# Evictions in three steps, a level of a head in two, a reordered first stage, and a gate pair as the stream's last, in a hybrid recurrent and convolutional layer

## The chip, the core and the metric

The kernel runs on one NeuronCore of a Trainium2 chip. The metric is the device time of one execution in microseconds. The core's engines work side by side, each through its own queue in the order of the program: TensorE (PE in the profile; its weight loads are PEld), VectorE (DVE), ScalarE (ACT) and GpSimd (POOL) compute, and SyncE (SP) issues most DMAs. An engine whose next instruction waits does not look past it.

## What is computed

One layer on a prompt of 1024 tokens with 16 meta tokens ahead of it, and on 8 single-token samples with a stored state. The reference, cut:

```python
xn = rmsnorm(h, norm_pre)
proj = xn @ w_in                       # 1024 x (10 * 1024), ten sections
q, fr, i_in, z_a, b_g, c_g, h_c, z_b, gate_a, gate_b = split(proj)
f = lb + (1 - lb) * sigmoid(fr);  k = 1 - f;  qa = silu(q)
# per head (8 heads, 128 x 128 state), exactly causal:
#   S_t = diag(f_t) S_{t-1} + k_t v_t^T ;  o_t = q_t^T S_t      (v = i_in)
o = o * rsqrt(mean(o * o) + EPS) * hgrn_norm * silu(z_a);  y_a = o @ w_a
u = c_g * h_c;  conv = causal conv of width 3 over u
y_b = (b_g * conv * silu(z_b)) @ w_b
merged = sigmoid(gate_a) * y_a + sigmoid(gate_b) * y_b
h = h + rmsnorm(merged @ w_o, norm_post)
```

Products are made to nearly float32 accuracy: each operand is split into a high part (ACT, a cast) and a low part (DVE or POOL, a subtraction), and a product is three matmuls, high x high, high x low, low x high (`mm3`, lines 112 to 116).

## The kernel before

**First stage (lines 850 to 1000).** The tokens come in eight chunks of 128, the even ones by SP, the odd ones by an indirect DMA that POOL issues (`load_chunk`). For a chunk c: `square(c)` on ACT and `rsqrt` on POOL (lines 82 and 83), `normalise(c)` on DVE, `turns(c)` (eight transposes on PE), `highs(c)` on ACT and `lows(c)` on DVE. They fill the factors b11, b12, b21, b22. Beside them the first head's input and forget projections are made in the plain way, four column ranges each (`plain`, 24 matmuls or `mm3` x 8; its evictions are e1 and e2). Then `sums12(i)` on DVE (eight subtractions, line 219) and `sums34(i)` on POOL make the differences that the other factors are turned from.

**The stream (`strassen`, line 544).** All other projections go in 39 pairs of sections, by a scheme of seven products for a 2 x 2 block product. A pair has products j = 0 to 6, each of two column chunks c, so 14 chunks of 12 matmuls; "chunk" below means one of these. After a chunk's matmuls `flush()` runs what was put off into the list `later`, then the weights' high part (c = 0, ACT) or low part (c = 1, DVE) of the product after next is made, and the chunk's own eviction `after(...)` is put into `later`: it is issued one chunk on. At j = 0, 2, 4 it copies the bank to a slot `sc` (ACT, line 554); at j = 1, 4, 5, 6 it calls the pair's `evac`, with the copy as `s`, or with none (j = 5). `added` sums bank and copy on DVE (line 281). Two banks `ga`, two `gb` and four `h` are there; product j = 0 of the next pair takes the `ga` banks that j = 5 leaves (odd pairs from 25 on take `h` banks).

The order of pairs is `stream_of`: query and output gate of head 0, then for each further head a pair of merge gates, input and forget, query and output gate; then the eighth gate pair, then for m = 0 to 7 a `u_pair(m)` and a `b_pair(m)` of the convolution branch. A u pair's `end` puts off the convolution's taps: ACT line 698, DVE lines 700 to 708, which run in the first chunks of the b pair behind it.

**What is woven in.** `weave` emits the steps of a generator between the chunks: a step of weight w comes once its middle falls due on the scale of chunks. `hgrn(m)`, the recurrence of a head, has 23 steps over 42 chunks (`W_HG`): preparation, seven levels of a scan over blocks that double (line 421 on: matmuls L424, then DVE `kc` L426, an ACT copy, `place_scores`, DVE `xc` L432 and a product L434), the states, and per half g `read_half(g)` (PE, ACT squares, `rsqrt` on POOL), `scaled(g)` (DVE L503), `back(g)` (four transposes, PE L509) and `gated(g)` (DVE L514). `add` (line 570), three POOL operations for the next pair's weights, is issued in a pair at j = 4. `sample_steps` then spreads the eight samples' work over the 176 chunks from pair 25 on, ten steps for each head: among them two DVE multiplications of 128 x 1024 (L778, L782), their sum (L784) with its output DMA, and one step later eight small matmuls on the sum (L790). In the last pair `tail` adds `fill`: it loads the recurrence's results and splits them (ACT and DVE, 128 x 1032 each).

**The rest** (line 1038 on): the products with w_a, w_b and w_o, and the output. The change leaves it alone.

Of the kernel before, what the change touches and what calls it, by code (L numbers as in the profile page):

```python
# [19 lines left out]
HL = 524  # L20
# [12 lines left out]
def hybrid_step(ctx: ExitStack, tc: tile.TileContext,  # L33
# [254 lines left out]

    def i_out(m, h, c0, n, pt, s):
        out = of_head(m, "it", h, c0, n)  # L290
        if s is None:
            act.copy(out, pt)
        else:
            added(pt, s, out)

    def f_out(m, h, c0, n, pt, s):
        out = of_head(m, "f", h, c0, n)
        sigmoid(added(pt, s, out), n, out)
        act.activation(out=out, in_=out, func=AF.Identity, scale=omlb[:, m:m + 1], bias=lb[:, m:m + 1])

    def q_out(m, h, c0, n, pt, s):
        out = of_head(m, "x", h, c0, n)
        y = added(pt, s)
        sg = sigmoid(y, n)
        later.append(lambda: (vec if s is None else pool).tensor_tensor(out=out, in0=y, in1=sg, op=ALU.mult))

    def z_out(m, h, c0, n, pt, s):
        out = of_head(m, "zs", h, c0, n)
        y = added(pt, s)
        sg = sigmoid(y, n)  # L310
        later.append(lambda: vec.scalar_tensor_tensor(out=out, in0=y, scalar=hnorm, in1=sg, op0=ALU.mult, op1=ALU.mult))  # L311


    W_HG = [0.8, 1.7, 1.7, 1.8, 1.4, 1.2, 1.9, 3.3] + [3.2] * 5 + [2.2] + [0.8, 0.8, 0.8, 1.9, 1.9, 1.2, 1.2, 1.2, 1.2]

    def hgrn(m):
# [13 lines left out]
        turned(iT, V, 0)  # L330
# [7 lines left out]
        turned(iT, V, 1)  # L338
# [4 lines left out]
        ex = slot("ex", 24)  # L343
        pool.tensor_copy(cap(ex, 0, [[12, 2], [1, 12]]), cap(iT, 512, [[HL, 2], [1, 12]]))
# [69 lines left out]
        for l in range(7):  # L414
# [38 lines left out]
        place_scores(6, got)  # L453
        turned(K, KT, 0)
# [73 lines left out]
        scaled(1, *r1)  # L528
        b0 = back(0)
# [14 lines left out]
    def strassen(pairs, tail):  # L544
# [5 lines left out]
        def after(j, c, c0, n, o, of_c, held, evac, end):  # L550

            cols = slice(c0, c0 + n)
            if j in (0, 2, 4):
                act.copy(held[j][:, cols], o)  # L554
            if j == 1:
                evac(0, 0, c0, n, o, held[0][:, cols])
            if j == 4:
                evac(1, 1, c0, n, of_c[:, 0:n], held[4][:, cols])
            if j == 5:
                evac(1, 0, c0, n, o, None)  # L560
            if j == 6:
# [153 lines left out]
    def b_pair(m):  # L715
        def evac(r, h, c0, n, pt, s):
            t = conv[m][:, HY * h + c0:HY * h + c0 + n]
            y = added(pt, s)
            if r == 0:
                vec.tensor_tensor(out=t, in0=t, in1=y, op=ALU.mult)  # L720
            else:
                sg = sigmoid(y, n)

                def rest():
                    vec.tensor_tensor(out=sg, in0=y, in1=sg, op=ALU.mult)
                    vec.tensor_tensor(out=t, in0=t, in1=sg, op=ALU.mult)
                later.append(rest)
# [8 lines left out]
    def gate_pair(sec, m, dst):  # L736
        def evac(r, h, c0, n, pt, s):
            out = slot("cs", HL - 256)[:, 0:n] if s is None else s
            sigmoid(added(pt, s), n, out)
            sync.dma_start(dst[m + r][:, HY * h + c0:HY * h + c0 + n], out)  # L740
# [24 lines left out]
    N_SAMPLE = 10  # L765

    def sample_steps():
        loaded = sample_state(0)
        for m in range(8):
# [15 lines left out]
            sync.dma_start(hgrn_s_out[0, :, m].rearrange("b k v -> k b v"), sin.rearrange("p (b v) -> p b v", b=8))  # L785
            yield
# [60 lines left out]
    stream_of += [gates[7]] + [f(m) for m in range(8) for f in (u_pair, b_pair)]  # L847
# [39 lines left out]
    load_chunk(5)  # L887
    square(2)
    load_chunk(7)
    normalise(0)  # L890
    turns(0)
    square(1)
    normalise(2)
    highs(0)
    turns(2)
    lows(0)
# [25 lines left out]
    for kk in range(2):  # L922
        w_high(rf, wf, kk)
        w_low(rf, wf, kk)
    square(3)
    normalise(1)
    e1 = plain(wi, 0, *C0)
    turns(1)
    normalise(3)
    highs(1)  # L930
    turns(3)
    lows(1)
    e2 = plain(wf, 0, *C0)
    square(4)
    normalise(4)
    highs(3)
    lows(3)
    e1()
    turns(4)
    square(6)  # L940
    normalise(6)
    highs(4)
    lows(4)
    e2()
    e1 = plain(wi, 1, *C0)
    turns(6)
    square("s", 24)
# [10 lines left out]
    turns(5)  # L958
    square(7)
    normalise(7)  # L960
    highs(5)
    lows(5)
    e2()
# [4 lines left out]
    small_parts(s22, t2)  # L968
    highs(7)
    lows(7)  # L970
    e2 = plain(wf, 0, *C1)
    for i in range(4):
        sums12(i)
    next(stream)
    for i in range(4):
        sums34(i)
    e1()
    turn(1, 1)
    turn(3, 1)
    e2()  # L980
    e1 = plain(wi, 1, *C1)
# [243 lines left out]
```

## Time and profile before

| | |
|---|---|
| median of 3 runs | 1319.78 us (1318.26 to 1321.21) |
| profiled execution | 1319.05 us, its span 1317.2 us |
| PE busy | 1260.4 us, 96% |
| DVE, ACT, POOL busy | 844.3, 534.7, 406.1 us |
| first matmul of the stream | 60.37 us after the span's start |
| last matmul of the stream | 1029.86 us |
| mean granted TensorE clock | 0.991 |

Times below are microseconds from the span's start. A matmul's end is modelled, so short gaps can lie inside its bar: two pairs of one kind are best compared by their whole lengths. A granted clock under 1.00 in a stretch is the share of full speed (2.4 GHz) on average; 0.50 is the lower level, 1.2 GHz.

### The profile page before, as it was taken

The page shows a single profiled execution, that of the slowest core. Times are in us where ns is not written, and L with a number is a line of the kernel's source. Part 1 is how long each engine was busy: PE and PEld are TensorE (multiplying, and loading weights), DVE is VectorE, ACT ScalarE, POOL GpSimd, SP SyncE. Part 2 cuts the span into 40 slices and gives each one's busy share as a digit, 9 for nine tenths or more (in the row PEclk, how much of TensorE's full clock was granted, in tenths as well). Part 3 has the DMA queues.
Part 4 walks back from the last instruction along what each step waited for, and adds up shares of the span by engine and source line. Part 5 has one row for each costly group of instructions (what it writes and reads, how often), then busy time and mean ns, then how long its engine had stood idle before and what let it go on. Part 6 is the DMA issues. An engine that isn't in the chain of part 4 may idle for free. (4 is left out here: it accounts for less than half of the span.)

```text
span 1317.2 us, 25325 instructions
## 1 busy us (share of the span) xinstructions
PE 1260.4 (96%) x10041; PEld 1221.6 (93%) x10041; DVE 844.3 (64%) x1412; ACT 534.7 (41%) x1280; POOL 406.1 (31%) x502
## 2 busy tenths in 40 slices
PE   6899999999999999999999999899998999999997
PEld 5789999999999999999999999899998999999876
DVE  5878586685858668585785777676576523546052
ACT  6454555555455545445543333333334312313031
POOL 5634242433324242342522544344344000000010
PEclk9899999999999999999999999899999999999999
DMA  7012031221203122130222434242326633522041
GB/s 219 9 48 76 27 105 41 63 69 59 82 27 97 49 59 73 46 94 28 79 60 78 149 96 137 64 138 81 112 71 209 222 97 98 177 96 83 16 162 56
DMA packets 146500, 117.11 MB, mean 89 GB/s; under 512 B 6641, under 2 KB 130650, under 8 KB 146382
## 3 DMA queue, kind: packets, MB, share of 16 engines
q1 hardware_dynamic: 145806, 113.40, 28.1%
q0 software_dynamic: 576, 2.10, 0.4%
q8 instruction: 79, 1.29, 0.4%
q14 instruction: 39, 0.32, 0.1%
HBM read 89.48 MB, written 25.96 MB: 88 GB/s over the span
## 5 line engine op out<-in xcount | busy, mean ns | idle before, releaser
L595 DVE TENSOR_TENSOR w<-wq,w 128x512 fp32r<-128x512 f32 x153 | 125.0, 817 | 28.2 <-ACT w L589 27.5
L589 ACT CAST w<-sm 128x512 fp32r<-128x512 f32 x117 | 72.1, 616 | 150.4 <-PE gb L116 126.7
L281 DVE TENSOR_TENSOR sc<-gb,sc 128x256 f32<-128x256 f32 (+1 forms) x144 | 60.2, 418 | 68.8 <-ACT sc L554 66.3
L595 DVE TENSOR_TENSOR w<-sm,w 128x512 fp32r<-128x512 f32 x117 | 84.1, 719 | 29.7 <-ACT w L589 29.7
L589 ACT CAST w<-wq 128x512 fp32r<-128x512 f32 x156 | 96.3, 618 | 15.7 <-PE h L116 14.6
L599 POOL TENSOR_TENSOR sm<-wq,sm 128x512 f32<-128x512 f32 x39 | 60.6, 1554 | 136.1 <-DVE w L595 118.2
L114 PE MATMUL gb<-s1h,w 128*128 128x256 f32 (+2 forms) x344 | 100.7, 293 | 0.0
L114 PE MATMUL gb<-s3h,w 128*128 128x256 f32 (+2 forms) x328 | 95.7, 292 | 3.6 <-DVE sc L281 2.5
L554 ACT COPY sc<-ga 128x256 f32<-128x256 f32 x192 | 71.7, 374 | 66.6 <-PE ga L116 65.1
L115 PE MATMUL gb<-s1l,w 128*128 128x256 f32 (+2 forms) x344 | 97.7, 284 | 0.0
L575 POOL TENSOR_TENSOR sm<-wq 128x512 f32<-128x512 f32 x39 | 57.7, 1481 | 120.7 <-DVE w L595 95.2
L114 PE MATMUL gb<-s6h,w 128*128 128x256 f32 (+2 forms) x328 | 94.4, 288 | 0.0
L1138 POOL TENSOR_TENSOR st<-st,half 128x1 f32<-128x1 f32 (+1 forms) x9 | 5.0, 551 | 286.8 <-DVE st L1136 283.9
L115 PE MATMUL gb<-s3l,w 128*128 128x256 f32 (+2 forms) x328 | 93.2, 284 | 0.0
L115 PE MATMUL gb<-s6l,w 128*128 128x256 f32 (+2 forms) x328 | 92.4, 282 | 0.0
L116 PE MATMUL gb<-s3h,w 128*128 128x256 f32 (+3 forms) x312 | 89.0, 285 | 1.6 <-DVE w L595 1.5
L116 PE MATMUL gb<-s1h,w 128*128 128x256 f32 (+3 forms) x312 | 88.7, 284 | 0.5 <-DVE w L595 0.5
L116 PE MATMUL gb<-s6h,w 128*128 128x256 f32 (+3 forms) x312 | 88.2, 283 | 0.0
L114 PE MATMUL ga<-s0h,w 128*128 128x256 f32 (+3 forms) x288 | 83.1, 289 | 1.2 <-DVE zs L311 1.2
L114 PE MATMUL ga<-s2h,w 128*128 128x256 f32 (+3 forms) x272 | 80.5, 296 | 2.1 <-ACT sc L554 2.1
L115 PE MATMUL ga<-s0l,w 128*128 128x256 f32 (+3 forms) x288 | 81.2, 282 | 0.0
L114 PE MATMUL ga<-s5h,w 128*128 128x256 f32 (+3 forms) x256 | 74.9, 293 | 3.8 <-ACT sc L554 1.7
(748 smaller groups left out, 4692.4 us busy)
## 6 DMA issues: line engine op xcount, KB each, us to landing
wq<-in_w_in_dram SPq DMA_DIRECT2D x160, 256.0 KB
oz<-zs SPq DMA_DIRECT2D x16, 258.0 KB
ob<-zs SPq DMA_DIRECT2D x8, 516.0 KB
x<-ga SPq DMA_DIRECT2D x8, 516.0 KB
x<-gb SPq DMA_DIRECT2D x8, 516.0 KB
wq<-in_w_a_dram SPq DMA_DIRECT2D x16, 256.0 KB
wq<-in_w_b_dram SPq DMA_DIRECT2D x16, 256.0 KB
wq<-in_w_o_dram SPq DMA_DIRECT2D x16, 256.0 KB
```

Source lines behind the costliest of these rows:

```text
L114: pe.matmul(pt, wh, xh, start=first, stop=False, skip_group_check=onto)
L115: pe.matmul(pt, wh, xl, start=False, stop=False, skip_group_check=onto)
L116: pe.matmul(pt, wl, xh, start=False, stop=last, skip_group_check=onto)
L281: vec.tensor_tensor(out=out, in0=pt, in1=s, op=ALU.add)
L554: act.copy(held[j][:, cols], o)
L575: pool.tensor_tensor(out=s3, in0=a11, in1=a21, op=ALU.subtract)
L589: act.copy(w[:, 0:512], source(i))
L595: (pool if j in pairs[p][2] else vec).tensor_tensor(out=w[:, 512:1024], in0=source(i), in1=w[:, 0:512].bitcast(F32), op=ALU.subtract)
L599: pool.tensor_tensor(out=s2, in0=raws[p, 0, 1], in1=s2, op=ALU.subtract)
L1138: pool.tensor_tensor(out=rs[0:rows], in0=rs[0:rows], in1=half[0:rows, 0:1], op=ALU.pow)
```

## The change

- **Three steps.** A new `silu` puts the sigmoid off by one more chunk and the multiplication by another one: sum, sigmoid and multiplication of an eviction now come in three successive flushes. It serves query, output gate and the b pairs' r = 1; the sigmoids of forget gate and merge gates (with their DMA) are put off by one chunk too. The query's multiplication, on POOL before, is on DVE. At j = 4, `evac` comes one chunk after the copy that it needs.
- **Heads.** A level is two steps: matmuls, `kc` and `place_scores`; then the copy, `xc` and L434. Both halves of V, and the small copy `ex`, come in the first step; the placing of the last level, and `back(0)`, are steps of their own. 32 steps with new weights.
- **Samples.** Eleven steps for a head: an empty one between the sum and the matmuls.
- **Order of the stream.** The eighth gate pair moves from ahead of the u and b pairs to the end.
- **First stage.** Squares are issued earlier, the odd chunks 5 and 7 are both loaded ahead of the second square, `normalise(1)` comes ahead of `lows(2)`, the lower bounds' small operations later, two of the four `sums12` ahead of a plain product.

```diff
+    def silu(y, n, use):
+        def first():
+            sg = sigmoid(y, n)
+            later.append(lambda: use(sg))
+        later.append(first)
...
     def f_out(m, h, c0, n, pt, s):
         out = of_head(m, "f", h, c0, n)
-        sigmoid(added(pt, s, out), n, out)
-        act.activation(out=out, in_=out, func=AF.Identity, scale=omlb[:, m:m + 1], bias=lb[:, m:m + 1])
+        y = added(pt, s, out)
+        def gate():
+            sigmoid(y, n, out)
+            act.activation(out=out, in_=out, func=AF.Identity, scale=omlb[:, m:m + 1], bias=lb[:, m:m + 1])
+        later.append(gate)
...
-        sg = sigmoid(y, n)
-        later.append(lambda: (vec if s is None else pool).tensor_tensor(out=out, in0=y, in1=sg, op=ALU.mult))
+        silu(y, n, lambda sg: vec.tensor_tensor(out=out, in0=y, in1=sg, op=ALU.mult))
...
-    W_HG = [0.8, 1.7, 1.7, 1.8, 1.4, 1.2, 1.9, 3.3] + [3.2] * 5 + [2.2] + [0.8, 0.8, 0.8, 1.9, 1.9, 1.2, 1.2, 1.2, 1.2]
+    W_HG = [2.6, 1.7, 1.7, 1.8, 1.4, 1.2, 1.9, 1.7, 1.9] + [2.2, 1.3] * 5 + [1.2, 1.2] + [0.6, 0.8, 0.8, 0.8, 1.9, 1.9, 1.2, 1.2, 0.8, 1.2, 1.2]
...
             vec.tensor_tensor(out=kc, in0=kc, in1=cap(eb, eo + 1, [[2, nb], [hb - 1, 2], [0, B]]), op=ALU.mult)
+            if l:
+                place_scores(l - 1, last)
+            yield
             if l < 6:
                 ko = 512 * ((l + 1) % 2)
                 act.copy(comp(kms, ko, nb // 2, 2 * B, 2 * B), comp(K, 0, nb // 2, HL + 2 * B, 2 * B))
-            if l:
-                place_scores(l - 1, last)
...
         scaled(1, *r1)
+        yield
         b0 = back(0)
...
             if j == 4:
-                evac(1, 1, c0, n, of_c[:, 0:n], held[4][:, cols])
+                later.append(lambda: evac(1, 1, c0, n, of_c[:, 0:n], held[4][:, cols]))
...
-    N_SAMPLE = 10
+    N_SAMPLE = 11
...
             sync.dma_start(hgrn_s_out[0, :, m].rearrange("b k v -> k b v"), sin.rearrange("p (b v) -> p b v", b=8))
+            yield
             yield
...
-    stream_of += [gates[7]] + [f(m) for m in range(8) for f in (u_pair, b_pair)]
+    stream_of += [f(m) for m in range(8) for f in (u_pair, b_pair)] + [gates[7]]
...
     square(0)
     load_chunk(5)
+    load_chunk(7)
     square(2)
-    load_chunk(7)
     normalise(0)
...
     highs(2)
+    normalise(1)
     lows(2)
+    square(3)
+    for kk in range(2):
+        w_high(rf, wf, kk)
+        w_low(rf, wf, kk)
+    e1 = plain(wi, 0, *C0)
...
+    square(5)
+    square(7)
+    e2()
+    flush()
     e2 = plain(wf, 1, *C0)
-    square(5)
     normalise(5)
     s11, s12, s21, s22 = turn_small()
     for b, to in ((s11, b11), (s12, b12), (s21, b21), (s22, b22)):
         small_parts(b, to)
+    normalise(7)
+    turns(5)
     e1()
...
     highs(7)
     lows(7)
+    for i in range(2):
+        sums12(i)
     e2 = plain(wf, 0, *C1)
-    for i in range(4):
+    turn(1, 1)
+    turn(3, 1)
+    for i in range(2, 4):
         sums12(i)
     next(stream)
```

## Rows read from the trace of the kernel before

**Rows 1.** The page, part 1: busy time and share of each engine

```profile
PE 1260.4 (96%) x10041; PEld 1221.6 (93%) x10041; DVE 844.3 (64%) x1412; ACT 534.7 (41%) x1280; POOL 406.1 (31%) x502
```

**Rows 2.** Windows: stretch, length, PE, PEld, DVE, ACT, POOL busy, clock, DMA

```profile
0.00:60.37 60.37, 42.21 (x282) 39.75 (x283) 42.37 (x54) 32.04 (x69) 34.84 (x45) 0.94 0.40 122
...
60.37:90.03 29.66, 26.57 (x226) 25.86 (x224) 21.08 (x37) 15.13 (x36) 12.62 (x13) 1.00 0.15 43
...
214.98:245.15 30.17, 29.17 (x244) 28.52 (x244) 16.48 (x34) 13.69 (x46) 9.92 (x10) 1.00 0.07 21
654.99:679.65 24.66, 24.66 (x211) 24.64 (x210) 21.77 (x35) 9.25 (x20) 8.65 (x13) 1.00 0.28 82
679.65:713.67 34.02, 30.97 (x245) 30.11 (x244) 22.68 (x46) 14.18 (x45) 10.31 (x17) 0.95 0.06 19
...
1001.44:1029.86 28.42, 21.61 (x171) 20.39 (x170) 23.11 (x37) 18.16 (x30) 7.27 (x18) 1.00 0.83 285
```

**Rows 3.** Windows, same columns: pairs 25, 27, 30, 32, 35, 36, 37

```profile
713.67:735.97 22.30, 21.15 (x186) 20.61 (x185) 13.86 (x25) 6.46 (x14) 7.00 (x7) 1.00 0.71 224
...
756.60:779.56 22.96, 21.87 (x189) 21.07 (x188) 15.86 (x28) 6.58 (x16) 7.03 (x5) 1.00 0.35 104
...
821.83:849.11 27.28, 23.23 (x188) 22.54 (x186) 18.55 (x32) 9.04 (x21) 9.61 (x14) 0.87 0.22 61
...
870.11:890.60 20.49, 20.49 (x176) 20.49 (x173) 15.79 (x29) 8.82 (x22) 9.60 (x15) 1.00 0.43 128
932.18:957.27 25.09, 22.81 (x190) 22.43 (x188) 13.42 (x27) 6.86 (x17) 7.27 (x6) 0.93 0.35 106
957.27:981.00 23.73, 21.54 (x187) 20.67 (x186) 20.32 (x32) 8.85 (x20) 10.20 (x17) 1.00 0.21 59
981.00:1001.44 20.44, 20.44 (x173) 20.44 (x172) 10.27 (x22) 6.46 (x15) 8.89 (x8) 1.00 0.36 113
```

**Rows 4.** Waits of PE: who waited for whom, total us, times, longest

```profile
PE h L509 <- DVE u L503: 7.3, 8, 0.9
PE h L790 <- DVE u L784: 6.3, 3, 4.1
...
PE h L790 <- DVE a L784: 2.3, 1, 2.3
...
PE h L327 <- DVE k L426: 2.1, 1, 2.1
```

**Rows 5.** Timeline of DVE in pair 24: first taps, and the head behind them

```profile
683.43 1.54 DVE L700 SCALAR_TENSOR_TENSOR zs<-x,vecs,zs 128x512 f32<-128x512 f32 x2 [2.02 <-ACT zs L698]
...
688.50 0.68 DVE L426 TENSOR_TENSOR k<-k,ee 128x512 f32<-128x512 f32 x1
```

**Rows 6.** Lines of DVE: group xcount | busy us, mean ns | idle before

```profile
L784 DVE TENSOR_TENSOR u<-u,v 128x1024 f32<-128x1024 f32 x4 | 6.0, 1488 | 0.0
```

**Rows 7.** Timeline, end of a head: start, length, engine, line, operation [idle before, releaser]

```profile
239.36 1.29 POOL L577 TENSOR_TENSOR sm<-wq 128x512 f32<-128x512 f32 x1
...
240.86 0.68 DVE L595 TENSOR_TENSOR w<-wq,w 128x512 fp32r<-128x512 f32 x1
...
241.11 1.33 POOL L83 TENSOR_TENSOR st<-st,half 128x4 f32<-128x4 f32 x1
...
242.47 0.69 DVE L503 TENSOR_TENSOR u<-h,st 128x512 f32<-128x512 f32 x1 [0.93 <-POOL st L83]
243.08 0.48 DVE L311 SCALAR_TENSOR_TENSOR zs<-ga,vecs,cs 128x256 f32<-128x256 f32 x1
...
243.22 0.66 PE L509 MATMUL h<-ident,u 128*128 128x128 f32 x4 [0.92 <-DVE u L503]
```

**Rows 8.** Timeline of POOL: the same power operation early in the first stage

```profile
5.96 0.58 POOL L83 TENSOR_TENSOR st<-st,half 128x1 f32<-128x1 f32 x1
```

**Rows 9.** Timeline of DVE, first stage: first and last of eight subtractions

```profile
44.32 0.68 DVE L219 TENSOR_TENSOR a<-a,u 128x512 f32<-128x512 f32 x1
...
55.14 1.65 DVE L219 TENSOR_TENSOR zs<-zs 128x512 f32<-128x512 f32 x1
```

More of the change, by code (lines that the diff above doesn't have):

```diff
@@ L309, in z_out @@
         y = added(pt, s)
-        sg = sigmoid(y, n)
-        later.append(lambda: vec.scalar_tensor_tensor(out=out, in0=y, scalar=hnorm, in1=sg, op0=ALU.mult, op1=ALU.mult))
-    W_HG = [0.8, 1.7, 1.7, 1.8, 1.4, 1.2, 1.9, 3.3] + [3.2] * 5 + [2.2] + [0.8, 0.8, 0.8, 1.9, 1.9, 1.2, 1.2, 1.2, 1.2]
+        silu(y, n, lambda sg: vec.scalar_tensor_tensor(out=out, in0=y, scalar=hnorm, in1=sg, op0=ALU.mult, op1=ALU.mult))
+    W_HG = [2.6, 1.7, 1.7, 1.8, 1.4, 1.2, 1.9, 1.7, 1.9] + [2.2, 1.3] * 5 + [1.2, 1.2] + [0.6, 0.8, 0.8, 0.8, 1.9, 1.9, 1.2, 1.2, 0.8, 1.2, 1.2]
     def hgrn(m):
@@ L328, in turned @@
             act.copy(to[:, 512 * g:512 * g + 512], pt)
-        turned(iT, V, 0)
+        for g in range(2):
+            turned(iT, V, g)
+        ex = slot("ex", 24)
+        pool.tensor_copy(cap(ex, 0, [[12, 2], [1, 12]]), cap(iT, 512, [[HL, 2], [1, 12]]))
         yield
@@ L337, in hgrn @@
         vec.tensor_tensor(out=cap(kms, 0, [[512, 2], [1, 512]]), in0=cap(K, 0, both), in1=cap(X, 0, both), op=ALU.mult)
-        turned(iT, V, 1)
         yield
@@ L342, in hgrn @@
         vec.tensor_tensor(out=cap(X, 0, both), in0=cap(X, 0, both), in1=cap(F, 0, both), op=ALU.mult)
-        ex = slot("ex", 24)
-        pool.tensor_copy(cap(ex, 0, [[12, 2], [1, 12]]), cap(iT, 512, [[HL, 2], [1, 12]]))
         yield
@@ L721, in evac, with rest @@
             else:
-                sg = sigmoid(y, n)
-                def rest():
+                def rest(sg):
                     vec.tensor_tensor(out=sg, in0=y, in1=sg, op=ALU.mult)
                     vec.tensor_tensor(out=t, in0=t, in1=sg, op=ALU.mult)
-                later.append(rest)
+                silu(y, n, rest)
         def end():
@@ L737, in evac, with gate @@
         def evac(r, h, c0, n, pt, s):
-            out = slot("cs", HL - 256)[:, 0:n] if s is None else s
-            sigmoid(added(pt, s), n, out)
-            sync.dma_start(dst[m + r][:, HY * h + c0:HY * h + c0 + n], out)
+            y = added(pt, s)
+            def gate():
+                out = slot("cs", HL - 256)[:, 0:n] if s is None else s
+                sigmoid(y, n, out)
+                sync.dma_start(dst[m + r][:, HY * h + c0:HY * h + c0 + n], out)
+            later.append(gate)
         return (sec_of(sec, m), sec_of(sec, m + 1)), chunks_of(HY), (), evac, lambda: None
@@ L785, in sample_steps @@
             sync.dma_start(hgrn_s_out[0, :, m].rearrange("b k v -> k b v"), sin.rearrange("p (b v) -> p b v", b=8))
+            yield
             yield
@@ L887, in hybrid_step @@
     load_chunk(5)
+    load_chunk(7)
     square(2)
-    load_chunk(7)
     normalise(0)
     turns(0)
-    square(1)
     normalise(2)
     highs(0)
+    square(1)
+    lows(0)
     turns(2)
-    lows(0)
     for kk in range(2):
@@ L900, in hybrid_step @@
     highs(2)
+    normalise(1)
     lows(2)
+    square(3)
[3 more added lines that the diff above has]
+    e1 = plain(wi, 0, *C0)
+    turns(1)
+    normalise(3)
+    highs(1)
+    lows(1)
+    square(4)
+    turns(3)
+    normalise(4)
+    square(6)
+    highs(3)
+    lows(3)
+    e2 = plain(wf, 0, *C0)
+    turns(4)
+    normalise(6)
+    e1()
+    highs(4)
+    lows(4)
     pvp = hbank()
@@ L921, in hybrid_step @@
     vec.tensor_scalar(out=omlb, in0=lb, scalar1=-1.0, scalar2=1.0, op0=ALU.mult, op1=ALU.add)
[L922 to L944, printed above, removed]
+    square("s", 24)
     e1 = plain(wi, 1, *C0)
     turns(6)
-    square("s", 24)
     normalise("s", 24)
@@ L956, in hybrid_step @@
         small_parts(b, to)
-    e1()
-    turns(5)
-    square(7)
-    normalise(7)
+    normalise(7)
+    turns(5)
+    e1()
     highs(5)
     lows(5)
-    e2()
     e1 = plain(wi, 0, *C1)
@@ L968, in hybrid_step @@
     small_parts(s22, t2)
+    e2()
+    flush()
     highs(7)
     lows(7)
+    for i in range(2):
+        sums12(i)
     e2 = plain(wf, 0, *C1)
-    for i in range(4):
+    turn(1, 1)
+    turn(3, 1)
+    for i in range(2, 4):
         sums12(i)
     next(stream)
[L975 to L981, printed above, removed]
     for c in (1, 3):
@@ L984, in hybrid_step @@
         turn_low(c, 1, t2)
+    e1()
+    for i in range(4):
+        sums34(i)
+    e1 = plain(wi, 1, *C1)
+    e2()
+    flush()
     turn(5, 1)
```

## The prediction

> **What bounds the kernel now.** I read the page's busy times first. PE is busy 96% of the span, DVE 64% [rows 1]: only idle PE time, or PE time at the lower clock, can be won; the change takes no matmul away. Then windows by stage [rows 2]: the first stage is 60.4 us with PE busy for 42.2 (the last part, after 1029.86, isn't touched). The stream is 39 pairs, and comparing pairs of one kind shows where the stream loses. Undisturbed, a u pair takes 20.44 and a b pair 20.49, PE busy throughout [rows 3], so a chunk is about 1.46 us. Five pairs of the convolution part take 22.30, 22.96, 27.28, 25.09 and 23.73: 121.36, against 3 x 20.44 + 2 x 20.49 = 102.30, so 19.1 lost. The last pair takes 28.42: 7.9 lost. Pair 24, the last third of head 7, takes 34.02, where the same third of another head takes 30.17 (the first seven agree within 0.1): 3.9 lost [rows 2]. Last I asked for PE's waits: 8.6 us are four waits of the sample matmuls for their sum, 7.3 are eight, one a head, of `back(1)` for `scaled(1)`, 2.1 is one of the last head's transposes [rows 4].
>
> **The convolution part (pairs 25 to 37).** Of the 19.1 lost, 8.6 are the sample matmuls' waits [rows 4]. The clock shares of 0.87 and 0.93 are time at the lower level: 0.13 x 27.28 + 0.07 x 25.09 = 5.3, and both pairs hold a long wait [rows 3]. That leaves 5.2 for late low parts and late bank sums. Before, the sum has one step of 176 / 80 = 2.2 chunks, 3.2 us, to be made; after, two steps of 176 / 88 = 2 chunks, 5.8 us. The longest wait, 4.1, would shrink to 1.5, the other three vanish, and with them most likely the dips. Eleven steps at two chunks also fix where DVE's sample work falls: head m starts at chunk 22m, its multiplications come after chunks 22m + 2 and 22m + 4, the sum after 22m + 6, the matmuls after 22m + 10. The taps come after chunks 28n + 1 and 28n + 2. Only m = 0 (chunks 2, 4, 6) and m = 5 (112, 114, 116 beside 113 and 114) fall on taps. There DVE is already full: in pair 24 it is held from 683.43 to 688.50 by the taps and one low part [rows 5]. A sum of 128 x 1024 takes 1.5 there [rows 6]; I count one for m = 0 and two for m = 5, and with the low parts behind them 2 + 3 = 5 us, plus 2 of small waits that stay. So 19 - 7 = **12 gained** (7 if dips and bank waits stay, 16 if the collisions are covered).
>
> **The last pair.** It loses 7.9 with DVE busy 23.1 and ACT 18.2 of 28.4 us [rows 2], because `fill` and the taps and multiplications of b pair 7 stand in the same queues as the copies that free banks. As the last pair a gate pair has no taps and no multiplications: some 4.4 us less on DVE for the taps (683.43 to 688.50 less a low part's 0.68 [rows 5, 7]), and a dozen multiplications of up to 0.48 [rows 7], about as much again; ACT keeps as many sigmoids as before. The u pair's tile `it`, which `fill` loads into, is also free a pair earlier. Its DMAs join SP's queue: each waits for its sigmoid, and weight loads of the next part stand behind it; those for the first product are issued earlier, so I cost it at nothing, at 1 us if not. I take **6 gained** (3 to 7.9).
>
> **Pairs 22 to 24.** The tap block of u pair 0 now meets levels 1 and 2 of head 7 in pair 23 instead of its last level in pair 24. Pair 23's DVE was busy 21.8 of 24.7 us without taps and without a b pair's multiplications [rows 2]; a b pair with its taps holds 15.79 - 10.27 = 5.5 more than a u pair [rows 3], so 27.3 of work stand against 24.7 of time. In pair 24 the head's `kc` stood 8.85 us after the pair's start because of the taps (688.50 - 679.65) [rows 5]; in pair 23 the matmuls of level 2 are due 6.7 us after it (four chunks and one level's 0.9), and need `xc` behind the same taps. The taps' first input now is at the front of DVE's queue, 1.3 us sooner, so the wait is between 1.4 and 2.8; I take 1.9. Pair 24's loss of 3.9, of which 0.05 x 34.02 = 1.7 is clock [rows 2], goes. **2 gained** (-1 if pair 23 loses the clock too; 3.9 if there is no wait).
>
> **The ends of the heads.** The wait of `back(1)`, 0.9 a head, goes back to POOL: `rsqrt` of the second half stands behind the three operations of `add`, then the power takes 1.33 beside a low part on DVE; `scaled(1)` starts at 242.47 and the transposes at 243.22 [rows 7]. The change doesn't move `back(1)`: it still comes after chunk 40 of 42. It moves `scaled(1)` one chunk up, ahead of the low part of chunk 39. DVE then stands still for POOL, and the power runs undisturbed, in 0.58 [rows 8]: `scaled(1)` starts some 0.75 sooner, by 241.7, and the wait shrinks to about 0.2. By the other bound, 1.33 again, half the wait stays. But what DVE did while it waited (the low part, a sum, a multiplication from a slot) now stands behind `scaled(1)`, and then `gated(0)`, before the multiplication L311 that frees the first `ga` bank for the next pair. With L311's 0.48 for the sum and each multiplication, and `scaled(1)`'s 0.69 for `gated(0)`, that is 0.69 + 0.68 + 2 x 0.48 + 0.69 + 0.48 = 3.5 us from 241.7, so 245.2 [rows 7]. PE is through with chunk 41 at about 244.3: the next pair began at 245.15 [rows 2], and I take off the 0.9 of the old wait. It waits 0.9 there and some 0.5 a chunk later. So **nothing gained**: the wait moves a chunk and a half on. Over seven heads the bounds are +6 (no new wait) and -6 (the whole of the new waits added).
>
> The Trainium skill's page "SBUF — State Buffer", section "Who interferes with whom", calls VectorE's and GpSimd's shared port pair an exclusive lock that is held for a whole instruction. The power's 1.33 beside the low part of 0.68, against 0.58, agrees [rows 7, 8]. The same rule speaks against the query's multiplications on DVE, where they can now block POOL, and each is some 0.4: by it alone the `rsqrt` chain would be no faster, and the heads would lose up to 0.5 each, 3.5 in all.
>
> **Levels in two.** The same DVE work in smaller portions. `xc` now has one chunk, 1.46 us, until the next level's matmuls at most levels, where three passed before. In the pairs that hold the levels DVE was busy 21.8 of 24.7 [rows 2], and PE never waited there: PE busy equals the length. Nothing (0 to -28, the rival below).
>
> **First pair (60.37 to 90.03).** PE idles 3.1 there [rows 2]. With sums and sigmoids in separate flushes ACT reaches the casts of factor 5 some 1 us sooner: **1 gained** (0 to 1.5).
>
> **First stage.** Its end hangs on eight subtractions of `sums12`, 44.32 to 56.79 [rows 9], that follow the last chunk's low parts; then one plain product, and the stream at 60.37. The first takes 0.68, the later ones 1.65 to 1.77 beside POOL's. The change keeps the eight in one run on DVE, behind the same low parts and beside the same POOL work. Squares and the second product's weights come sooner, but the first head's sigmoid now stands on ACT ahead of the copies of the small tokens, on which the next product waits. Both move what is ahead of 44.32 by a microsecond either way: **nothing** (-2 to +2).
>
> **Sum.** 12 + 6 + 2 + 0 + 0 + 1 + 0 = 21 from the profiled execution of 1319.05: 1298.05. The median is 0.73 above that execution, so 1298.8.
>
> **The rivals.** *The waits only move* (chance 0.20): taps, sample work and a b pair's multiplications keep DVE as the limit at the start of each b pair, pair 23 loses the clock, and the last pair stays bound by `fill`. For it: DVE is busy 18.6 to 23.1 us in the disturbed pairs [rows 2, 3]. Against it: the undisturbed b pair has the same taps at 15.8 busy and loses nothing. It gives 5 + 3 - 1 + 0 = 7 to 9: about 1311.
>
> *The heads and the first stage give too* (0.14): the `ga` banks come free in time, 6, and the first stage 2, 4 more from collisions that are covered: 33 in all, 1287.
>
> *Slower, by the levels in two* (0.07): the place is the next level's matmuls behind `xc`, the price 0.7 for each of 40, 28 us, which after the 21 gained gives about 1327. It decides from the point where DVE is more than one chunk, 1.46 us, behind when `xc` is issued. Against it: PE busy equals the length in pair 23 [rows 2].
>
> *Nothing to be seen* (0.04): gains and new waits cancel, 1317 to 1322.
>
> **How the numbers follow.** The forecast, 1298.8, has 0.55, with 1292 to 1306 as its own range from the bounds of its terms taken together by half. The range of 8 in 10 takes in most of the first two rivals: 1287 to 1312. A measurement of this kernel can tell about 0.2%, 2.6 us. Faster: 0.55 + 0.20 + 0.14 = 0.89; same 0.04; slower 0.07.
>
> **What would show it.** Right: sample matmuls gone from PE's waits or down to one, pairs 25 to 37 at 20.4 to 23 with two longer ones (m = 0 in pair 25, m = 5 in pair 33, at taps), the last pair under 23. `back(1)` down to 0.2 a wait, and in its place a wait of the first `ga` matmul of the next pair for a DVE multiplication. A wait at level 2 in pair 23. A stream that starts within 2 us of 60.4. Wrong: waits of L424 for L432 all over the heads, half clock in new places, or a first stage that is several us shorter.

## The result, and the profile after

The changed kernel takes 1332.6 us (median; 1332.2 to 1334.2), the kernel before 1319.7: a ratio of 1.010 with a 95% interval of 1.008 to 1.012, so 13 us slower. The forecast was 1298.8 and the range 1287 to 1312. The profiled execution took 1334.2 with a span of 1332.1, against 1319.05 and 1317.2.

Page of the changed kernel, part 1; it answers to [rows 1]:

```profile
PE 1268.3 (95%) x10041; PEld 1224.9 (92%) x10041; DVE 843.9 (63%) x1444; ACT 535.3 (40%) x1280; POOL 383.6 (29%) x470
```

The same matmuls, and DVE with the same busy time (844.3 before), though the query's 32 multiplications came to it: what PE lost is waits and low clock. POOL, which gave them up, is busy 22.5 us less. Windows of the changed kernel, columns as in [rows 2] (length, busy time of PE, PEld, DVE, ACT, POOL, clock, DMA share, GB/s): first stage; first pair; the three pairs of one head; pairs 23, 24, 25; pairs 33 and 35; the last pair:

```profile
0.00:60.78 60.78, 41.64 (x282) 39.11 (x282) 41.39 (x54) 32.46 (x70) 35.90 (x45) 0.94 0.39 122
60.78:90.45 29.67, 26.58 (x226) 25.93 (x225) 19.82 (x39) 14.51 (x35) 11.51 (x11) 1.00 0.15 42
247.77:270.72 22.95, 22.71 (x183) 22.25 (x184) 18.40 (x28) 13.51 (x29) 8.04 (x12) 1.00 0.34 104
270.72:295.93 25.21, 25.08 (x211) 24.89 (x210) 20.92 (x32) 12.39 (x28) 8.73 (x10) 1.00 0.25 74
295.93:326.52 30.59, 29.38 (x246) 28.51 (x244) 15.75 (x35) 13.76 (x46) 8.03 (x8) 1.00 0.07 21
664.75:697.80 33.05, 27.38 (x212) 27.08 (x210) 29.12 (x47) 11.38 (x25) 11.38 (x22) 0.90 0.12 33
697.80:728.64 30.84, 29.79 (x245) 28.75 (x244) 16.52 (x36) 11.20 (x39) 8.04 (x8) 1.00 0.12 38
728.64:754.32 25.68, 23.06 (x186) 22.13 (x185) 20.78 (x36) 8.87 (x20) 10.24 (x16) 0.93 0.62 185
...
902.89:927.91 25.02, 22.91 (x188) 22.19 (x187) 18.35 (x32) 8.88 (x20) 8.99 (x14) 0.93 0.23 65
948.25:969.48 21.23, 21.23 (x189) 20.79 (x188) 15.35 (x31) 9.01 (x22) 10.36 (x15) 1.00 0.36 100
1011.00:1045.28 34.28, 23.97 (x170) 22.88 (x169) 20.51 (x30) 18.34 (x31) 5.15 (x9) 0.85 0.65 219
```

Lengths of the stretches, from their first matmuls, against the same stretches before:

| stretch | before | after | difference | forecast |
|---|---|---|---|---|
| first stage | 60.37 | 60.78 | +0.4 | 0 |
| pair 0 | 29.66 | 29.67 | 0 | -1 |
| pairs 1 to 22 (heads 0 to 6, a third of head 7) | 564.96 | 574.30 | **+9.3** | 0 |
| pairs 23 and 24 | 58.68 | 63.89 | **+5.2** | -2 |
| pairs 25 to 37 | 287.77 | 282.36 | -5.4 | -12 |
| pair 38 | 28.42 | 34.28 | **+5.9** | -6 |
| the rest | 287.34 | 286.82 | -0.5 | 0 |
| span | 1317.20 | 1332.10 | +14.9 | -21 |

Each length is from one trace, and traces differ where nothing was changed: pair 24 of the old order takes 32.5 to 34.0, its pairs 25 to 37 take 286.5 to 289.1, and the last pair of the new order 31.9 to 32.8 in four runs whose edits leave it alone, against 34.3 here. So of the +5.9 some 2 are this execution's own. The heads' pairs mostly agree within 0.1.

The waits of PE in the changed kernel (who waited for whom: total us, times, longest), against [rows 4]. L320 is the output gate's multiplication (311 before), L433 and L442 a level's matmuls and `xc` (424 and 432), L520 `back`, L566 the copy of a bank to its slot:

```profile
PE ga L114 <- ACT sc L566: 8.8, 2, 8.5
PE ga L114 <- DVE zs L320: 8.2, 15, 2.1
...
PE h L433 <- DVE x L442: 6.4, 5, 5.7
PE h L520 <- DVE u L514: 4.1, 8, 0.5
```

The sample matmuls' 8.6 are gone, as forecast, and three of `back`'s 7.3. In their place stand three waits of which the kernel before had little: one of 8.5 for a copy on ACT, fifteen for L320, one of 5.7 for a level.

### The profile page after: what moved, and what is told of

It reads as the page before. It is cut to its first block, busy times and chain, and to the rows that moved or that the text cites. A ratio compares the mean times of both kernels' runs of the same rounds, so it can differ in the third digit from the quotient of the medians.

```text
span 1332.1 us, 25269 instructions
## 1 busy us (share of the span) xinstructions
PE 1268.3 (95%) x10041; PEld 1224.9 (92%) x10041; DVE 843.9 (63%) x1444; ACT 535.3 (40%) x1280; POOL 383.6 (29%) x470
## 3 DMA queue, kind: packets, MB, share of 16 engines
q8 instruction: 79, 1.29, 0.4%
## 5 line engine op out<-in xcount | busy, mean ns | idle before, releaser
L566 ACT COPY sc<-ga 128x256 f32<-128x256 f32 x192 | 71.9, 375 | 100.7 <-PE ga L116 98.1
L601 ACT CAST w<-wq 128x512 fp32r<-128x512 f32 x156 | 97.2, 624 | 23.4 <-PE ga L116 12.1
L587 POOL TENSOR_TENSOR sm<-wq 128x512 f32<-128x512 f32 x39 | 66.3, 1699 | 111.5 <-DVE w L607 92.8
L607 DVE TENSOR_TENSOR w<-sm,w 128x512 fp32r<-128x512 f32 x117 | 83.4, 713 | 22.1 <-ACT w L601 22.0
L114 PE MATMUL ga<-s4h,w 128*128 128x256 f32 (+3 forms) x256 | 73.9, 289 | 8.5 <-ACT sc L566 8.5
```

Source lines behind the costliest of these rows:

```text
L114: pe.matmul(pt, wh, xh, start=first, stop=False, skip_group_check=onto)
L587: pool.tensor_tensor(out=s3, in0=a11, in1=a21, op=ALU.subtract)
L601: act.copy(w[:, 0:512], source(i))
L607: (pool if j in pairs[p][2] else vec).tensor_tensor(out=w[:, 512:1024], in0=source(i), in1=w[:, 0:512].bitcast(F32), op=ALU.subtract)
```

## The experiments

The kernel before ran beside all experiments; its medians were 1319.7 to 1320.2. "Pairs" are lengths from the trace as in the table above.

### Which part costs: one part alone on the kernel before

**The order of the stream alone.**

```diff
-    stream_of += [gates[7]] + [f(m) for m in range(8) for f in (u_pair, b_pair)]
+    stream_of += [f(m) for m in range(8) for f in (u_pair, b_pair)] + [gates[7]]
```

> The kernel before with the last gate pair at the stream's end, nothing else. Theory (the order alone brings both new stalls): pair 23 stalls at a level of head 7 behind the taps, by 4 to 9, pair 24 gives 3 to 4 back, and the last pair is 2 to 6 longer, since the loads for the next part stand behind stores on SP's queue: 1323 to 1332. Rival (the order only hurts together with evictions in three steps, which put the stores off): pair 23 as forecast, 2, the last pair 3 to 6 shorter: 1312 to 1317.

1321.4, ratio 1.0007 (0.9997 to 1.0016): no change in sum, and two large ones inside it. The last pair grows from 28.4 to 40.1; pairs 25 to 37 shrink from 287.77 to 279.82; pair 23 grows by 3.8 and pair 24 gives 3.5 back. Both expectations missed the total, since neither had the gain in the convolution. The stalls belong to the order, without three steps:

```profile
992.74:1032.81 40.07, 26.30 (x170) 24.99 (x169) 21.42 (x31) 18.50 (x32) 5.71 (x9) 0.79 0.58 199
653.96:682.42 28.46, 25.73 (x212) 24.86 (x210) 25.14 (x44) 10.70 (x24) 10.48 (x19) 1.00 0.10 29
```

**The heads' new steps and weights alone** (`W_HG`, a level in two, the step between `scaled(1)` and `back(0)`).

```diff
             vec.tensor_tensor(out=kc, ...)
+            if l:
+                place_scores(l - 1, last)
+            yield
             if l < 6:
...
         scaled(1, *r1)
+        yield
         b0 = back(0)
```

> The kernel before with the heads' new steps and weights alone. Theory (the 1.3 us that each head loses are the three steps of the evictions, not the heads): the wait of back(1) falls from 0.9 to some 0.4 a head, no new wait, 1315 to 1319. Rival (levels in two, or scaled(1) ahead, cost it): each head 0.5 to 1.3 longer, 1323 to 1329.

1327.7, ratio 1.0052 (1.0036 to 1.0068). The rival holds: a head's second pair, the one with the slow levels, goes from 24.8 to 26.2, its third from 30.2 to 29.9, the first pair behind it from 22.45 to 22.6, so a head loses 1.1 to 1.2. Waits of PE, and the timeline of two levels (start, length, engine, line, operation, [idle before, releaser]):

```profile
PE h L424 <- DVE x L433: 6.6, 16, 0.7
```

```profile
195.69 2.51 DVE L402 COPY_PREDICATED a<-masks,h 128x512 f32<-128x512 uint8 x1
...
197.81 0.91 DVE L598 TENSOR_TENSOR w<-sm,w 128x512 fp32r<-128x512 f32 x1
...
198.63 0.68 DVE L433 TENSOR_TENSOR x<-x,ee 128x512 f32<-128x512 f32 x1
...
199.46 0.35 PE L424 MATMUL h<-x,u 128*128 128x128 f32 x1 [0.62 <-DVE x L433]
...
202.18 1.32 DVE L402 COPY_PREDICATED a<-masks,h 128x512 f32<-128x512 uint8 x1
...
205.11 0.35 PE L424 MATMUL h<-x,u 128*128 128x128 f32 x1 [0.24 <-DVE x L433]
```

`xc` (L433) now starts a step later, behind the 2.51 of `place_scores` and a low part, and the next level's matmuls are due one chunk on. There are 16 such waits of 0.4 on average, two a head: 0.3 to 0.7 behind the first copy of a head, which takes 2.51, and 0.2 behind the second, which takes 1.32. The other three copies take 0.74, and nothing waits there. This is the rival that had a chance of 0.07, at two levels a head in place of five.

**The eleventh sample step alone.**

```diff
-    N_SAMPLE = 10
+    N_SAMPLE = 11
```

(with the empty step ahead of the sample matmuls)

> The kernel before with the eleventh sample step alone. Theory (the step does what was forecast): the four waits of the sample matmuls, 8.6 us, go and one part of the half clock with them; sample work falls on taps at m = 0 and m = 5, which costs 4 to 5 in each of the two pairs, as in the changed kernel, where pairs 25 and 33 lose 5.3 and 4.5. Pairs 25 to 37 lose 15 to 18 in place of 22.8, so 1313 to 1316. Rival (the gain in these pairs is due to the order or to the three steps): within 2 of 1319.7.

1318.2, ratio 0.9983 (0.9970 to 0.9996): 2 us, as the rival has it. The four waits of the sample matmuls do vanish from its list of waits, and pair 35 falls from 25.09 to 21.62; but pairs 25 to 37 still take 286.48, no less than in a trace where they are unchanged (286.50 in `first_only`, below), since pair 25 loses 3.3 and pair 28 1.7. The reason for pair 25 is plain in DVE's waits. In the kernel before, then with eleven steps:

```profile
DVE a L778 <- DMA a<-in_state_hgrn_dram: 4.2, 1, 4.2
```

```profile
DVE a L778 <- DMA a<-in_state_hgrn_dram: 6.2, 1, 6.2
```

and PE's with eleven steps:

```profile
PE gb L114 <- DVE it L676: 2.7, 1, 2.7
```

With more steps in the same stretch the first multiplication comes sooner, and waits in DVE's queue for its state to land; the sum that frees a bank (L676) stands behind it, and PE waits 2.7 and then runs at the lower clock: pair 25 is 25.64 long at a mean clock of 0.93.

**The first stage alone.**

```diff
-    square(1)
     normalise(2)
     highs(0)
+    square(1)
...
+    for i in range(2):
+        sums12(i)
     e2 = plain(wf, 0, *C1)
-    for i in range(4):
+    turn(1, 1)
+    turn(3, 1)
+    for i in range(2, 4):
         sums12(i)
```

> The kernel before with the reordered first stage alone. Theory (its end hangs on the eight subtractions behind the last chunk's low parts, which the reordering keeps): the stream starts within 1 of 60.4 and the time is within 2 of 1319.9. Rival (the reordered stage gains or loses several us that another part of the change hid): 1314 to 1317, or 1323 to 1326.

1320.4, ratio 1.0008 (0.9998 to 1.0019), as the theory had it.

### The changed kernel without the three steps

```diff
-        silu(y, n, lambda sg: vec.tensor_tensor(out=out, in0=y, in1=sg, op=ALU.mult))
+        sg = sigmoid(y, n)
+        later.append(lambda: (vec if s is None else pool).tensor_tensor(out=out, in0=y, in1=sg, op=ALU.mult))
```

(and so for the forget gate, the output gate, the b and gate pairs and the flush at j = 4)

> The changed kernel with evictions in two steps as before, all else as changed. Theory (three steps cost the heads' time, since multiplications and sigmoids that free banks come later): seven heads get back 1 each and the last pair 2 to 4, so 1319 to 1325. Rival (order and heads hold the loss): 1329 to 1333.

1336.6, ratio 1.0127 (1.0103 to 1.0151). Neither expectation holds: three steps help in this company, by 4 us (alone on the kernel before they weren't tried). With them the last pair is 34.3 in place of 39.3, but the heads gain nothing: the waits for `xc` shrink, and those for L320 come. (That last pair is this one trace's; see above how far it varies.) The other four parts, run alone, add up to 1.3 + 7.5 - 2.0 + 0.4 = 7, where together they cost 16.5. Most of the rest is pairs 23 and 24: order and heads each make pair 24 some 4 shorter when alone (3.5 and 4.1), and still only 3 together, while pair 23 grows by 3.8 and 1.35 alone and 7.8 together.

### The last pair

**The stores put off.** The gate pair's stores from slots go to SP four chunks later.

```diff
+    def put_off(f, n):
+        later.append((lambda: put_off(f, n - 1))) if n else f()
...
                 sigmoid(y, n, out)
-                sync.dma_start(dst[m + r][:, HY * h + c0:HY * h + c0 + n], out)
+                store = lambda: sync.dma_start(dst[m + r][:, HY * h + c0:HY * h + c0 + n], out)
+                wait = 4 if dst is gb_d and m == 6 and s is not None else 0
+                put_off(store, wait)
```

> The changed kernel with the last gate pair's stores from slots put off by four more chunks, past the loads of fill. Theory (SP's queue): as with the loads ahead, though the loads themselves are no earlier than their call: 1324 to 1328. Rival (DMA engines full, or the slots' release): 1331 to 1337.

**The loads issued ahead.** `fill` loads its first five tiles at its first call.

```diff
...
+        for k in (range(5) if src is oz_d and 0 in ks else ks):
+            if src is oz_d and k in ahead:
+                continue
+            t = ahead[k] = slot(RAWS[k % 5], NY)
+            sync.dma_start(t, src[k])
...
         for k in ks:
-            raws[k] = slot(RAWS[k % 5], NY)
-            sync.dma_start(raws[k], src[k])
...
+            raws[k] = ahead[k]
```

> The changed kernel with the first five loads of fill issued together at the first of its calls, ahead of the gate pair's stores on SP's queue. Theory (the last pair waits for loads that stand behind stores on SP's queue, which themselves wait for sigmoids): the last pair 34.3 goes to 23 to 27, 1321 to 1326. Rival (the loads are late since the DMA engines are full there): 1331 to 1335.

Stores put off: 1325.4 (ratio 1.0035, 1.0023 to 1.0048), the last pair 25.0, as its theory had it. Loads ahead: 1328.2 (1.0057, 1.0041 to 1.0074), the last pair 29.7: between theory and rival, since the loads behind the first five stay where they were, and PE waits 5.4 for what hangs on the sixth. Both go the way of the queue. The changed kernel's timeline of the last pair, from SP's queue to PE (L753 is a store of the gate pair, L96 a weight load of the next part, L842 a load of `fill`, L844 and L90 its copy and cast, L566 the copy that frees a bank):

```profile
1016.09 4.55 SPq L96 DMA_DIRECT2D wq<-in_w_a_dram  x2
...
1021.39 0.41 ACT L286 ACTIVATE sc<-sc 128x256 f32<-128x256 f32 x1
...
1021.83 0.34 SPq L753 DMA_DIRECT2D gb<-sc  x1
...
1023.66 0.32 SPq L753 DMA_DIRECT2D gb<-sc  x1
1024.33 0.32 SPq L842 DMA_DIRECT2D ee<-oz  x1
...
1030.89 0.19 POOL L844 COPY ee<-smpz 128x8 f32<-128x8 f32 x1 [10.50 <-DMA ee<-oz]
...
1031.12 1.05 ACT L90 CAST s2h<-ee 128x1032 fp32r<-128x1032 f32 x1 [3.19 <-POOL ee L844]
...
1034.47 0.37 ACT L566 COPY sc<-ga 128x260 f32<-128x260 f32 x1
...
1034.89 0.58 PE L114 MATMUL ga<-s4h,w 128*128 128x260 f32 x1 [8.52 <-ACT sc L566]
```

Read from the bottom: PE waits 8.52 for a copy on ACT; ACT has two casts of `fill` ahead of it, and the first waits for the load of `ee`; that load went out at 1024.33. From 1016.09 on SP stood for a weight load, 3.7 until its buffer was free, then for two stores, 1.1 and 0.4 until their sigmoids were done, and between them 0.6 for a load of the b results. With the stores put off it goes out 8 us sooner in its pair, and not the stores alone follow it, but the weight loads too:

```profile
1017.11 0.42 SPq L847 DMA_DIRECT2D ee<-oz  x1
...
1024.07 1.83 SPq L756 DMA_DIRECT2D gb<-sc  x2
1025.96 0.99 SPq L96 DMA_DIRECT2D wq<-in_w_a_dram  x2
```

So the queue is the cause; what of it is the stores' and what the weight loads', which moved with them, these two runs don't part.

### The heads, and pair 23

**Two steps for results that are read from their bank.** Product j = 5 has no slot, so its multiplication is what frees the bank.

```diff
-        later.append(first)
+        if bank:
+            first()
+        else:
+            later.append(first)
```

(`bank` is `s is None`, in q_out, z_out and the b pair)

> The changed kernel with two steps, as before, for the results that are read straight from their bank (product 5), three steps for the others. Theory (the wait of the next pair's first matmuls for zs, 8.2 us in all, is the third step of these): that wait goes, heads 0.7 to 1.2 shorter, 1324 to 1328. Rival (it is scaled(1) and gated(0) ahead of it on DVE): the wait stays over 5, 1330 to 1333.

1324.1, ratio 1.0035 (1.0023 to 1.0048): 8.5 gained on the changed kernel, as the theory had it; pairs 1 to 22 take 566.5, 7.8 less. A head's third pair goes from 30.6 to 29.8 and the pair behind it from 22.95 to 22.6. The wait for that multiplication:

```profile
PE ga L114 <- DVE zs L323: 1.5, 1, 1.5
```

**Whole levels.**

```diff
             if l:
                 place_scores(l - 1, last)
-            yield
             if l < 6:
```

(weights added)

> The changed kernel with a level of a head in one step again (weights added), all else as changed. Theory (a level in two puts its subtraction-side factor xc one chunk later, so PE waits for it): the waits at the levels, 0.3 to 1.3 a head, and most of pair 23's 5.9 with its half clock go: 1320 to 1326. Rival (the waits are the three steps' and the taps'): 1330 to 1333.

1329.7, ratio 1.0070 (1.0053 to 1.0086): 3 gained, between the two. Pairs 1 to 22 take 571.5, 2.8 less. The heads' second pairs are back at 24.84 each, 0.4 a head; pair 23 falls from 33.05 to 29.99, but pair 24 grows from 30.84 to 33.56 with half clock in it. The wait in pair 23 as the changed kernel has it, on DVE (L435 `kc`, L411 `place_scores`, L712 taps, L442 `xc`) and PE:

```profile
668.13 1.22 DVE L435 TENSOR_TENSOR k<-k,ee 128x512 f32<-128x512 f32 x1 [1.16 <-POOL ke L450]
...
669.27 2.52 DVE L411 COPY_PREDICATED a<-masks,h 128x512 f32<-128x512 uint8 x1
...
671.36 1.72 DVE L712 SCALAR_TENSOR_TENSOR zs<-x,vecs,zs 128x512 f32<-128x512 f32 x2
...
673.60 2.41 DVE L712 SCALAR_TENSOR_TENSOR zs<-x,vecs,zs 128x512 f32<-128x512 f32 x2
...
676.60 0.69 DVE L442 TENSOR_TENSOR x<-x,ee 128x512 f32<-128x512 f32 x1
...
677.44 0.55 PE L433 MATMUL h<-x,u 128*128 128x128 f32 x1 [5.67 <-DVE x L442]
```

`kc` and `xc` of one level stand 8.5 us apart, with the masks and both blocks of taps between them, since the level's second half is issued behind the taps. With whole levels `xc` starts at 672.05, ahead of the second block, and the longest wait for it is 2.1.

**The second block of taps three chunks later.**

```diff
-            later.append(lambda: (taps(0), later.append(lambda: (taps(1), sample_taps()))))
+            later.append(lambda: (taps(0), later.append(lambda: (sample_taps(), put_off(lambda: taps(1), 3)))))
```

> The changed kernel with the second block of a convolution's taps issued three chunks later than the first (the small sample taps go ahead of it). Theory (the 5.9 us wait in pair 23 is one level's xc queued on DVE behind both blocks of taps): pair 23 goes from 33.0 to 26 to 30, pairs 25 and 33 lose less too: 1322 to 1328. Rival (DVE simply has more work than time in pair 23, wherever the taps stand): 1331 to 1334.

1328.9, ratio 1.0068 (1.0047 to 1.0089): 3.7 gained, just short of the theory's range. Pair 23 only falls to 31.0, where 26 to 30 were expected, and pair 33 to 23.4; pair 25 gets longer by 1.8.

### Pairs 25 to 37

**The banks of the u and b pairs as the new order has them,** on the kernel before.

```diff
-            spare = p % 2 and p >= FREE_H
+            spare = p % 2 == 0 and p > FREE_H
```

> The kernel before with its u and b pairs' banks as they are after the change of order: from pair 26 on the even pairs (the b pairs) take h banks for product 0 in place of the odd ones. The order alone made pairs 25 to 37 8 us shorter. Theory (that gain is the taps, which hold DVE while the next product waits for ga banks: with h banks the b pairs need not wait): 4 to 8 us gained, 1312 to 1316. Rival (the gain is the sample steps' place against the taps, which this doesn't move): within 3 of 1319.8.

1319.0, ratio 0.9998 (0.9984 to 1.0011); pairs 25 to 37 take 289.02. The banks are not where the gain comes from.

**The sample work five chunks later,** on the kernel before, ten steps as there.

```diff
+    for _ in range(5):
+        next(stream)
     weave(stream, 14 * 13 - 6, sample_steps(), [1] * (8 * N_SAMPLE))
```

> The kernel before with the sample work begun five chunks later, same density, ten steps to a head. Theory (what the change of order gave pairs 25 to 37 is the place of the sample work against the taps: in the kernel before, heads m = 3 and m = 7 of the samples fall on taps, at chunks 71 and 155; five chunks later m = 3 comes behind them, and only m = 4, at 99, meets taps with its sum): the waits of the sample matmuls, 8.6, fall to under 4 and pairs 25 to 37 gain 4 to 8 of their 22.8: 1312 to 1316. Rival (the gain of the order came from elsewhere): within 2.5 of 1319.9.

1311.6, ratio 0.9932 (0.9915 to 0.9949). A little more than the theory had. Windows of pairs 25 to 37, in the kernel before, in this one, and in the one with the order alone:

```profile
713.67:1001.44 287.77, 276.39 (x2338) 271.31 (x2337) 196.00 (x342) 99.19 (x229) 121.20 (x147) 0.98 0.37 111
```

```profile
712.57:993.11 280.54, 274.04 (x2338) 268.97 (x2337) 193.56 (x342) 99.14 (x229) 119.44 (x147) 0.99 0.37 114
```

```profile
712.92:992.74 279.82, 272.99 (x2338) 267.85 (x2337) 201.15 (x346) 101.62 (x235) 126.07 (x156) 1.00 0.39 117
```

Five chunks of shift, with neither the order nor the eleventh step, give 7.2 of the 8.0 us that the order gives there. The waits for the sums fall from 8.6 to 3.3. Pair 35 falls from 25.09 to 21.0, pairs 30 and 36 by 4.0 and 3.2. Pair 32, where head 4 of the samples now meets taps, gets worse by most, from 20.49 to 25.32; pairs 26 and 29 lose 2.3 and 1.5.

**Ten steps in the changed kernel.**

```diff
-    N_SAMPLE = 11
+    N_SAMPLE = 10
```

> The changed kernel with ten steps to a head of the samples. Theory (the pairs of the convolution gained from the change of order, which moved the taps by a pair against the sample work, and not from the eleventh step): pairs 25 to 37 lose 14 to 18 as now: 1330 to 1334. Rival (the eleventh step is what gained): waits for the sums are back, 1336 to 1342.

1331.2, ratio 1.0089 (1.0070 to 1.0108): not slower than with eleven; pairs 25 to 37 take 280.75 against 282.36. The theory holds: in the new order the eleventh step gains nothing.

### Four edits together

> The changed kernel with four edits together: whole levels, two steps for results read from the bank, the second block of taps three chunks later, the last pair's stores four chunks later. Theory (the losses lie in separate places and add): 1332.6 less 7 (stores), 7 (bank), 3 (levels), 4 (taps): 1310 to 1316. Rival (each freed wait comes back as another): 1320 to 1326.

`joined` is the changed kernel with whole levels, two steps for results read from a bank, the second taps later and the stores put off: 1305.4, ratio 0.9896 (0.9877 to 0.9914), 27 below the changed kernel and 14 below the one before, better than both expectations. The single gains add up to 7.2 + 8.5 + 2.9 + 3.7 = 22.3. Its pairs 23, 24 and 38:

```profile
652.63:682.62 29.99, 25.89 (x212) 24.91 (x210) 26.24 (x46) 10.69 (x24) 10.63 (x22) 1.00 0.13 36
682.62:712.50 29.88, 29.29 (x246) 28.64 (x245) 17.31 (x38) 11.49 (x40) 8.01 (x8) 1.00 0.12 39
991.84:1016.45 24.61, 21.22 (x171) 20.30 (x169) 19.36 (x29) 17.06 (x31) 4.32 (x9) 1.00 0.80 275
```

Against the kernel before, pairs 0 to 22 take 2.6 less, 23 and 24 1.2 more, 25 to 37 8.4 less and the last pair 3.8 less. With whole levels alone pair 24 had half clock; here both pairs run at full clock, 3.7 less. That is most of the 4.9 by which the four together beat the sum.

The same with ten sample steps:

> The four edits together on the changed kernel (1305.4), and ten steps to a head of the samples again. Theory (the eleventh step is worth nothing there): 1303 to 1306. Rival (it is needed once the other losses are gone): 1307 to 1312.

1305.2, ratio 0.9897 (0.9881 to 0.9914). The eleventh step is worth nothing in either place.

## Why the prediction was wrong, point by point

**The last pair (-6, was +5.9).** The step that failed is "Its DMAs join SP's queue ... I cost it at nothing, at 1 us if not". The working had only weights of the next part, behind the stores; in the trace two weight loads, two stores and a load of the b results stand ahead of `fill`'s load of `ee`, which goes out 8 us after SP came to the first of them, and PE waits 8.5 for what hangs on it. So the term was 9 us of queueing short in this trace, 7 in the medians. With the queue cleared the pair takes 25.0, 3.4 less than before, near the lower bound of the 3 to 7.9. The saving on DVE was over-sized too: it is busy 20.5 in place of 23.1 [rows 2], where the working took off some 9 for taps and multiplications.

**The heads (0, was +9.3).** Two steps failed. "Levels in two: nothing" read pair 23's cover (PE busy equals the length) as room for a whole chunk of 1.46; but at the first level of each head `place_scores` alone takes 2.51, with `xc` behind it and the next level's matmuls one chunk on. Alone the heads' steps cost 1.1 a head. The rival for it had the mechanism and the place; its price, 0.7 for each of 40 levels, 28 us, was about four times the 7.5 of `heads_only`, since only two levels of five pay, and its chance was too small. In the head's end the direction was right: `back`'s wait fell, from 0.9 to 0.5, and the first `ga` matmuls of the next pair wait in its place. But the working put the third step's own delay of the freeing multiplication at nothing, and charged the wait to what stands ahead of it on DVE: `bank_two` takes the third step out with `scaled(1)` left as it is, and 8.5 us go. The end-of-head sum also began wrongly, at a power of 0.58 "undisturbed": in the changed kernel DVE is idle beside it, and it takes 1.04. Both rows of the changed kernel:

```profile
321.98 1.04 POOL L83 TENSOR_TENSOR st<-st,half 128x4 f32<-128x4 f32 x1
...
323.05 0.69 DVE L514 TENSOR_TENSOR u<-h,st 128x512 f32<-128x512 f32 x1 [4.40 <-POOL st L83]
```

[Rows 8] is the power on one column, this one on four: the size sets 0.46 of the 0.75 that was put down to VectorE's work beside it. The Trainium skill's page "SBUF — State Buffer", section "Who interferes with whom", on the lock of the shared port pair, can account for 1.33 less 1.04 at most. The kernel before has both cases: seven such powers that begin inside a low part take 1.32 to 1.33, while eight inside which a low part begins take 1.04 to 1.05. Those low parts take their usual 0.68, so the rule of a lock held for the whole instruction is borne out by the first case and not by the second, as far as POOL's rough spans tell.

**Pairs 23 and 24 (-2, was +5.2).** The place was right, one level of head 7 behind u pair 0's taps in pair 23, and pair 24 gives 3.2 of its 3.9 back. The wait of 1.4 to 2.8 was mis-sized: it is 5.7, and the half clock behind it costs 3.3 more (0.10 of 33.05), which the working had only among its bounds. The working let `xc` pass as one operation behind the taps; with the level in two it has the masks (2.52) and both blocks (1.72 and 2.41) ahead of it. Of the 8.4 that pair 23 grows by, the order alone gives 3.8 (28.46), and whole levels take 3.1 off again (29.99); the rest isn't set apart.

**Pairs 25 to 37 (-12, was -5.4).** Which pairs would be hit was right: 25 and 33, but they lose 5.2 and 4.5 where 2 and 3 were taken. The working sized these new collisions and never the old ones. By the same count the old order has two as well, heads 3 and 7 in pairs 30 and 36, which took 27.28 and 23.73 [rows 3]: 51.0 together, against 50.7 for pairs 25 and 33 now. So the collisions moved and cost the same. What is gained is mostly pair 35, 25.09 before and 21.23 after. In the kernel before, the sum of head 6 stands on DVE there behind the b pair's last multiplications, and PE waits for it:

```profile
936.12 1.22 DVE L784 TENSOR_TENSOR a<-a,ee 128x1024 f32<-128x1024 f32 x1
...
937.48 0.65 PE L790 MATMUL h<-a,kt 128*32 128x128 f32 x16 [2.28 <-DVE a L784]
```

The clock is 0.66 and 0.50 in the next two stretches of 2 us. That loss was read rightly, and the eleventh step alone does take it away; but so do the order alone and the shift of five chunks (22.1 and 21.0), and the step pays for it in pairs 25 and 28. The cause of the gain was wrong: it was put down to the eleventh step; alone that gives these pairs no more than one trace differs from another, and taking it out of the changed kernel doesn't lengthen them. What gives is where the sample work meets the convolution's work on DVE: the order shifts them by a pair against each other, and a shift of five chunks in the kernel before does nearly the same.

**Pair 0 (-1, was 0) and the first stage (0, was +0.4)** were right within 1 us each.

**The rivals.** That waits only move (1311), and that levels in two are too slow (1327), each held a part of what happened, and that 1327 lies nearest to 1332.6 is luck: its price was wrong, and most of the loss came from elsewhere. A case in which several such waits come together had no chance of its own.

## What to carry to other kernels

A step moved into another place brings its queue with it: list for each queue what stands ahead of each load there, stores and loads of a later part included, before its work is counted as saved. Splitting a step doesn't make its second half cheaper; it puts it behind whatever is issued between. So look up the price of that at every size (here 2.51, 1.31 and 0.74 for one copy), and split only where the half that waits is not on the way to the next matmul, and never delay the operation that hands a bank back. And before a gain is put down to more slack, work out the collisions of the old schedule as carefully as those of the new one: here a shift of phase was worth 7 to 8 us, and a step of slack 2 at most.

## What the runs showed of the hardware

The power on POOL goes by its columns: in the median 0.57 us for one, 1.04 for four, 1.67 for eight, with the same 128 partitions (the changed kernel's line 83: count, then least, median and most in ns, shapes mixed):

```profile
L83 POOL TENSOR_TENSOR st<-st,half x25: 558/1036/1047, 5.8 to 724.9; 128x4 f32<-128x4 f32 x16, 128x1 f32<-128x1 f32 x8, 24x1 f32<-24x1 f32 x1
L83 POOL TENSOR_TENSOR so<-so,half x8: 1665/1672/1951, 765.3 to 1001.2; 128x8 f32<-128x8 f32 x8
```

`place_scores`, one predicated copy of 128 x 512 on DVE, goes by the blocks that it writes, not by its size. At a head's first level, in blocks of one element, it takes 2.50 to 2.52 us in the kernel before and in the changed one; at the second, in blocks of two, 1.29 to 1.33; at the next three, in blocks of 4 to 16, 0.72 to 0.76. It is so in all eight heads, with POOL at work beside it (before) or not (seven heads of the changed kernel).

A load of 516 KB, `ee`, issued at 1024.33 in the changed kernel with three more behind it, was there at 1030.84; from 1027 to 1031 the DMA engines were 99% busy at 356 GB/s. No run here timed such a load alone.
